# Moving ScalarE's transfers to GpSimd's queue and joining the attention's row loads into one broadcast transfer per operand

## The chip, the cores and the metric

One NeuronCore of a Trainium2 chip runs the whole kernel. The metric is the device time of one execution in microseconds (us); the number for a kernel is the median of its runs. In the names of the profile PE is the matrix engine, DVE is VectorE, ACT is ScalarE, POOL is GpSimd and SP is the SyncE engine, which here only issues transfers. A name with a q behind it (SPq, ACTq, POOLq) is that engine's instruction queue, which also issues the engine's transfers. The transfers themselves run on 16 DMA engines.

## What is computed

One inference step of a decoder layer on 1024 prompt rows and 64 sample rows (8 sequences of 8): a half feed-forward block, a mixing layer, and a second half feed-forward block. The mixing layer joins two parts: softmax attention of 12 heads of width 64, and a gated linear attention. Cut to what matters here (prompt rows):

```python
def _mix_prompt(h, ...):
    qa, ka, va, qb, kb, vb, rb, gk = _project(h, w_in, q_gain, k_gain, w_gk2, b_gk)
    for window, dil in DILATED_BRANCHES:           # (128,1), (512,4), (2048,16)
        o, l = _dilated_prompt(qa, ka, va, rel_bias, window, dil)
    oa = _merge_branches(outs, lses)
    ob, s_fin = _gla(qb, kb, vb, gk, s0, math.gcd(S, GLA_CHUNK))
    y = _merge_out(oa, ob, rb, gla_gain, w_out)
```

The kernel computes the three merged branches of a head as one softmax over all earlier rows, with a bias that holds the relative bias and the count of branches that see a row.

## The kernel before

The program runs in five stages. Times are those of the profiled execution: the first feed-forward block (0 to 788), norms and the projections of the mixing layer with the sample's attention beside them (to about 1244), the prompt's attention with the states of the linear attention beside it (to 1519), the output projection (to 1612), and the second feed-forward block (to the end).

All activations lie transposed, 128 features on the partitions, and every float32 product is made of three products of a high and a low part (`hH`, `hL` and the weights' `hl`). In the projection stage `inputs` runs over 25 units of weights; `turn_values`, `finish_qk` and `finish_gate` bring each unit's result into memory: values to `out_vp`, queries to `qsc`, keys to `out_kT`, the gate to `gsc`. Beside it `sample` computes the sample rows' attention and writes `wk` and `osc`. Before the change SP issues all loads, GpSimd the stores of `qsc` and `out_kT` (L473), and ScalarE all other stores of this stage (L434 to L446, L817, L907).

In `attention` the inner function `load(h)` (L918) brings one head's operands. Each of the query rows (`qsc`) and key rows (`out_kT`) of a head is a block of 64 rows of 1024 numbers, and each is needed twice, on partitions 0 to 63 and on 64 to 127 of a tile `f`:

```python
for w in range(2):
    nc.sync.dma_start(out=f[u][64 * w : 64 * w + 64], in_=src[64 * h : 64 * h + 64])
```

`f` has two buffers, so one for queries and one for keys: the queries of the next head can be loaded only when this head's have been read. VectorE then casts `q` (L932) and `kk` (L934), and GpSimd takes the low parts (L933, L935; VectorE does it for head 0). `bias` comes from `Z` (L937), with two buffers, and `va` (L940) for two heads at a time. `scores` multiplies `kk` by `q` (`psS`, L962) and VectorE makes `e` from it (L969), twelve such instructions a head. `linear_states` loads `g` and `gr` (L596, L598, L643).

Every engine works its instructions off in order. Which order that is, a scheduler decides when the program is built: the generators are interleaved by the costs that they yield (`_interleave`), and the scheduler then places each instruction by its own account of time. Pools that are closed give their memory to later tiles, so a first load of the attention can wait for the last reader of an older tile: `bias` of head 0 lies where the last weights of the projections were, and waits for the last matmul that reads them. Beside such waits a transfer that SP or ACT issues takes one of eight semaphores in turn (DMAHW0 to DMAHW7), and GpSimd's one of eight others (DMASW0 to DMASW7): an issue also waits until the transfer that held its semaphore before has landed.

`sbias` in `sample` (L799) is loaded in the form that the change gives to `f`: 16 rows of memory, repeated 8 times as the leading dimension of the source, onto 128 partitions.

Of the kernel before, what the change touches and what calls it, by code (L numbers as in the profile page):

```python
# [9 lines left out]
F32 = mybir.dt.float32  # L10
# [6 lines left out]
P = 128  # L17
NT = 1088
NP = 1024
# [101 lines left out]
class _Kernel:  # L121
# [299 lines left out]
    def turn_values(self, pool, ps, z, m, ci):  # L421
        nc, a = self.nc, self.a
        cols = slice(128 * m, 128 * m + 128)
        t0, nt = 3 * ci, 3 if ci < 2 else 2
        p = ps.tile([P, 512], F32, tag="b", name="psv")
        for t in range(nt):
            nc.tensor.transpose(p[:, 128 * t : 128 * t + 128], z[:, 128 * t : 128 * t + 128], self.ident)
        if ci == 2:
            nc.tensor.transpose(p[:64, 256:384], z[:, 256:320], self.ident)
        v = pool.tile([P, 3, 128], F32, tag="t1", name="v", bufs=4)  # L430
        nc.scalar.copy(v[:, :nt].rearrange("p t c -> p (t c)"), p[:, : 128 * nt])
        if ci == 2:
            nc.scalar.copy(v[:64, 2], p[:64, 256:384])
            nc.scalar.dma_start(out=self.vnew[:, cols], in_=v[:64, 2])  # L434
            nc.scalar.dma_start(
                out=a["wv_s"].rearrange("b (r c) -> b r c", c=768)[:, 2040:2048, cols], in_=v[:64, 2]
            )
            self.vdone = m + 1
        nc.scalar.dma_start(
            out=a["vp"][128 * t0 : 128 * (t0 + nt), cols].rearrange("(t p) c -> p t c", p=P), in_=v[:, :nt]  # L440
        )

    def finish_gate(self, z, m, ci):
        nc = self.nc
        nc.scalar.activation(z, z, AF.Silu)
        nc.scalar.dma_start(  # L446
            out=self.gsc[3 * ci : 3 * ci + 3, :, 5 + m].rearrange("t p r -> p t r"),
            in_=z.rearrange("p (t r) -> p t r", t=3),
        )
# [131 lines left out]
    def linear_states(self, pool, ps):  # L581

        nc, a = self.nc, self.a
        st = pool.tile([P, 9, 64], F32, tag="st", name="st", bufs=2)
        nc.gpsimd.memset(st[:, 0], 0.0)
        ms = pool.tile([P, 3, 36], F32, tag="gms", name="gms")
        qm = []
        for z in range(2):
            t = pool.tile([P, 4, 8, 32], F32, tag="qm", name="qm", bufs=2)
# [46 lines left out]
        for T in range(9):  # L636
# [11 lines left out]
            for j, src in enumerate((kdT, g[:, 3], g[:, 4])):  # L648
# [3 lines left out]
                out=kx,  # L652
# [125 lines left out]
    def sample(self, pool, ps, loadk):  # L778
# [18 lines left out]
        for i in range(6):  # L797
# [8 lines left out]
            for e in range(2):  # L806
# [9 lines left out]
            nc.scalar.copy(ko, p[:64, :128])  # L816
            nc.scalar.dma_start(  # L817
                out=a["wk"].rearrange("b (r c) -> b r c", c=768)[:, 2040:2048, 128 * i : 128 * i + 128], in_=ko
# [87 lines left out]
            for e in range(2):  # L906
                nc.scalar.dma_start(  # L907
                    out=self.osc[i, 64 * e : 64 * e + 64].rearrange("p (b t) -> p b t", t=8), in_=t[:, :, e]
                )
# [3 lines left out]

    def attention(self, inputs, pool, ps):
        nc = self.nc
        heads = {}

        def load(h):  # L918
            i, e = h // 2, h % 2
            f = []  # L920
            for u, src in enumerate((self.qsc, self.a["kT"])):
                f.append(inputs.tile([P, NP], F32, tag="f", name="f", bufs=2))
                if u == 0:
                    q = inputs.tile([P, NP], F32R, tag="q", name="q", bufs=2)
                    b = inputs.tile([P, NP], F32, tag="bias", name="bias", bufs=2)
                    kk = inputs.tile([P, 2, NP], F32R, tag="kk", name="kk", bufs=2)
                    kh, kl = kk[:, 0], kk[:, 1]
                for w in range(2):
                    nc.sync.dma_start(out=f[u][64 * w : 64 * w + 64], in_=src[64 * h : 64 * h + 64])
            o = slice(64, 128)  # L930
# [6 lines left out]
            nc.sync.dma_start(out=b, in_=bass.AP(z.tensor, z.offset + 127, [[GW - 1, P], [1, NP]]))  # L937
            if e == 0:
                v = pool.tile([P, 8, 128], F32, tag="v", name="va", bufs=2)
                nc.sync.dma_start(  # L940
                    out=v, in_=self.a["vp"][:, 128 * i : 128 * i + 128].rearrange("(t p) c -> p t c", p=P)
                )
            else:
                v = heads[h - 1][3]
            heads[h] = (q, kh, kl, v, b)

        def scores(h, g):

            q, kh, kl, v, b = heads[h]
            out = []  # L950
# [58 lines left out]
        def weigh(h, g, es, pts):  # L1009
            i, e = h // 2, h % 2  # L1010
            r = slice(64 * e, 64 * e + 64)
            v = heads[h][3]
            if g % 2 == 0 and e == 0:
# [26 lines left out]
        self.tc.keep_in_program_order(nc.scalar.preload_act_table_set(LOG_EXP))  # L1040
        load(0)
        yield 10
# [104 lines left out]
    def run(self):  # L1147
        nc, tc, a = self.nc, self.tc, self.a
        self.gready, self.done, self.vdone = False, 0, 0
        with ExitStack() as top:  # L1150
            self.dram = top.enter_context(tc.tile_pool(name="dram", bufs=1, space=DRAM))
# [121 lines left out]
            with ExitStack() as hs:  # L1273
                hpool(hs)
                with ExitStack() as bs:
# [3 lines left out]
                    states = (4.6 * c for c in self.linear_states(gp, ps0))  # L1279
                    _interleave(tc, [(self.attention(ip, ap, ps0), 0), (states, 0)])  # L1280
                with pool("wts") as wp, pool("xp", side="right") as xp:
# [165 lines left out]
```

## Time and profile before

| what | value |
|---|---|
| median of 3 runs | 2398.7 us (2397.25 to 2399.25) |
| the profiled execution's own time | 2401.93 us |
| its span, first to last instruction | 2400.1 us |
| mean granted clock of the matrix engine | 0.989 |
| PE busy over the span | 98% |
| VectorE, ScalarE, GpSimd busy | 48%, 27%, 17% |
| matrix engine's share of the chain that ended last | 89% |

The span is what the trace covers; the execution's own time is 1.8 us longer. The busy shares are averages over five stages, and the change touches only the second and third of them, about a quarter of the span. So the rows below are of those two stages alone.

### The profile page before, as it was taken

Reading aid. Unit: us, or ns where it says so; the run is one execution under the profiler, and the core shown is the slowest. Engines: PE = TensorE matmul, PEld = TensorE weight load, DVE = VectorE, ACT = ScalarE, POOL = GpSimd, SP = SyncE. Lnnn points to the kernel's source line nnn. Section 1 sums busy time; section 2 is a strip of 40 time slices with the busy share of each in tenths; the row PEclk is TensorE's granted clock in tenths of the full one; section 3 lists DMA queues with packets and bytes.
Section 4 is the critical chain, followed back from the end, with each engine's and each line's share of the span. In section 5 each row is a group of like instructions: output and inputs, shape, how many; then the busy total and the mean of one; then the engine's idle time right before and its main releaser. Section 6 shows DMA issues by size and latency. Waiting matters only on the chain.

```text
span 2400.1 us, 38321 instructions
## 1 busy us (share of the span) xinstructions
PE 2341.4 (98%) x16073; PEld 2215.0 (92%) x16073; DVE 1155.9 (48%) x2377; ACT 656.9 (27%) x1347; POOL 408.3 (17%) x303
## 2 busy tenths in 40 slices
PE   7999999999999998999989999999999999999999
PEld 6999999999999987978767767999999999999999
DVE  8452434344342753555538887435444342434333
ACT  5111020101101522545436666334111101020110
POOL 5011020101100400011103231333101101020100
PEclk9999999999999999999999999999999999999999
DMA  7346542524250334599865442414244243111002
GB/s 258 110 162 192 191 152 97 210 97 153 86 196 23 134 131 108 179 342 341 310 184 130 111 115 74 156 36 158 88 163 153 92 154 143 45 53 45 28 17 85
DMA packets 135261, 330.25 MB, mean 138 GB/s; under 512 B 25920, under 2 KB 105264, under 8 KB 127408
## 3 DMA queue, kind: packets, MB, share of 16 engines
q1 hardware_dynamic: 116464, 316.39, 38.7%
q10 hardware_dynamic: 16512, 5.11, 0.9%
q0 software_dynamic: 2112, 6.29, 0.7%
q8 instruction: 126, 2.06, 0.3%
q14 instruction: 47, 0.39, 0.0%
HBM read 300.55 MB, written 134.56 MB: 181 GB/s over the span
## 4 chain that ended last, share of the span: by engine, by line
PE 89%; DVE 5%; DMA 3%; ACT 2%; issue 1%; SPq 1%; POOL 0%; ACTq 0%; DVEq 0%; POOLq 0%
PE ps L306 42%; PE ps L257 21%; PE psg L306 12%; PE pso L306 4%; PE psO L1022 2%; PE psS L962 2%; PE psW L880 1%; PE psT L1001 1%; DMA vt<-in_vin 1%; PE psA L831 1%; DVE hL L155 1%; DVE e L969 1%; PE pss L459 1%; DMA f<-out_kT 0%; DVE rstd L170 0%
## 5 line engine op out<-in xcount | busy, mean ns | idle before, releaser
L306 PE MATMUL ps<-hH,hl 128*128 128x362 f32 (+1 forms) x4224 | 1044.1, 328 | 8.1 <-ACT hl L130 6.8
L306 PEld LDWEIGHTS ps<-hH,hl 128*128 128x128 f32 x4224 | 746.6, 188 | 12.4 <-ACT hl L130 6.7
L306 PE MATMUL ps<-hL,hl 128*128 128x362 f32 (+1 forms) x2112 | 691.5, 328 | 2.9 <-DVE hL L155 2.9
L257 PE MATMUL ps<-g,hl 128*128 128x362 f32 (+1 forms) x3168 | 529.2, 328 | 0.0
L257 PEld LDWEIGHTS ps<-g,hl 128*128 128x128 f32 x3168 | 527.0, 188 | 0.0
L134 POOL TENSOR_TENSOR hl<-raw,hl 128x1024 fp32r<-128x1024 f32 (+1 forms) x98 | 242.8, 2498 | 1223.3 <-ACT hl L130 1223.3
L306 PEld LDWEIGHTS ps<-hL,hl 128*128 128x128 f32 x2112 | 397.5, 188 | 4.9 <-DVE hL L155 3.9
L306 PE MATMUL psg<-hH,hl 128*128 128x384 f32 (+3 forms) x1200 | 312.4, 334 | 0.0
L262 DVE SCALAR_TENSOR_TENSOR xT<-ps,xT 128x362 f32<-128x362 f32 (+1 forms) x384 | 204.6, 534 | 200.3 <-PE ps L257 191.4
L217 ACT ACTIVATE t<-t 128x364 f32<-128x364 f32 x132 | 66.9, 508 | 786.0 <-DVE t L216 785.8
L218 DVE TENSOR_TENSOR t<-ps,rstd 128x364 f32<-128x364 f32 x132 | 70.6, 535 | 417.9 <-PE ps L306 417.9
L306 PEld LDWEIGHTS psg<-hH,hl 128*128 128x128 f32 (+1 forms) x1200 | 211.3, 186 | 12.8 <-issue 8.9
L306 PE MATMUL psg<-hL,hl 128*128 128x384 f32 (+3 forms) x600 | 200.1, 334 | 0.1
L130 ACT CAST hl<-raw 128x1024 fp32r<-128x1024 f32 (+2 forms) x148 | 124.1, 886 | 187.3 <-PE ps L306 109.9
L130 ACT CAST g<-t 128x364 fp32r<-128x364 f32 x132 | 65.2, 494 | 346.8 <-DVE t L219 346.8
L134 DVE TENSOR_TENSOR g<-t,g 128x364 fp32r<-128x364 f32 x132 | 107.1, 813 | 92.8 <-ACT g L130 92.5
L216 DVE TENSOR_TENSOR t<-ps,rstd 128x364 f32<-128x364 f32 x132 | 70.5, 535 | 156.6 <-PE ps L306 155.3
L306 PEld LDWEIGHTS psg<-hL,hl 128*128 128x128 f32 (+1 forms) x600 | 111.7, 186 | 9.3 <-issue 6.7
L134 DVE TENSOR_TENSOR hl<-raw,hl 128x384 fp32r<-128x384 f32 (+3 forms) x178 | 102.9, 587 | 23.9 <-ACT hl L130 19.9
L962 PE MATMUL psS<-kk,q 128*128 128x512 f32 (+2 forms) x288 | 92.2, 411 | 19.6 <-DVE s L969 11.9
L306 PE MATMUL pso<-hH,hl 128*128 128x362 f32 (+1 forms) x384 | 93.6, 325 | 0.2 <-DVE o L1032 0.2
L982 ACT ACTIVATE e<-e,s 128x128 f32<-128x128 f32 (+3 forms) x96 | 74.9, 780 | 43.7 <-DVE s L969 43.1
(205 smaller groups left out, 2007.2 us busy)
## 6 DMA issues: line engine op xcount, KB each, us to landing
out_wk<-in_ck SPq DMA_DIRECT2D x16, 3060.0 KB
out_wv_s<-in_cv SPq DMA_DIRECT2D x16, 3060.0 KB
kt<-in_kin SPq DMA_DIRECT2D x24, 1280.0 KB
vt<-in_vin SPq DMA_DIRECT2D x60, 512.0 KB
raw<-in_w13b SPq DMA_DIRECT2D x22, 1024.0 KB
raw<-in_w13a SPq DMA_DIRECT2D x21, 1024.0 KB
raw<-in_w2a SPq DMA_DIRECT2D x48, 192.0 KB
raw<-in_w2b SPq DMA_DIRECT2D x48, 192.0 KB
```

Of the source, the lines that this page charges most:

```text
L130: nc.scalar.copy(hi, x)
L134: e.tensor_tensor(out=lo, in0=x, in1=hi.bitcast(F32), op=ALU.subtract)
L155: nc.vector.scalar_tensor_tensor(out=self.hL[:, k, s], in0=x, scalar=g, in1=self.hH[:, k, s].bitcast(F32), op0=ALU.mult, op1=ALU.subtract)
L216: nc.vector.tensor_tensor(out=t1[:, :n], in0=p1[:, :n], in1=r, op=ALU.mult)
L217: nc.scalar.activation(t1[:, :n], t1[:, :n], AF.Silu)
L218: nc.vector.tensor_tensor(out=t3[:, :n], in0=p3[:, :n], in1=r, op=ALU.mult)
L257: self.mm(p[:, :n], lhsT=hl[:, wt, j, :], rhs=g[:, gp, :n], start=i == 0, stop=i == 3 * nf - 1)
L262: nc.vector.scalar_tensor_tensor(out=xs, in0=p[:, :n], scalar=0.5, in1=xs, op0=ALU.mult, op1=ALU.add)
L306: self.mm(p[:m, :n], lhsT=hl[:, wt, k, cs], rhs=h[:, k, h0 : h0 + n], start=i == 0, stop=i == 23)
L962: self.mm(p[:, :mm], lhsT=q[:, 128 * n : 128 * n + 128], rhs=kk[:, o : o + mm], start=x == 0, stop=x == 1,)
L982: nc.scalar.activation(e[:, :w], e[:, :w], AF.Exp, scale=-1.0, bias=s[:, j : j + 1], accum_out=s[:, 2:3])
L1022: self.mm(p[64 * n : 64 * n + 64, :128], lhsT=v[:, k, r], rhs=pts[k // 2][k, n], start=k == 0, stop=k == 2 * g + n, tile_position=(0, 64 * n),
```

## The change

Every transfer that ScalarE issued is now issued by GpSimd: 54 of them (18 of `out_vp`, 6 each of `vnew`, `out_wv_s`, `out_wk` and `gsc`, 12 of `osc`). In `load(h)` the two transfers of an operand become one whose source repeats the 64 rows: in the built program the source's dimensions are [2 (step 0), 64, 1024] and the destination's [128, 1, 1024]. The loads of `va` move into `load_v`, their tile into the pool of the linear states, the first one ahead of the states' work. Head 0's load is recorded with a higher priority, and the states are interleaved ahead of the attention.

```diff
--- before.py
+++ after.py
@@ -431,19 +431,19 @@
         nc.scalar.copy(v[:, :nt].rearrange("p t c -> p (t c)"), p[:, : 128 * nt])
         if ci == 2:
             nc.scalar.copy(v[:64, 2], p[:64, 256:384])
-            nc.scalar.dma_start(out=self.vnew[:, cols], in_=v[:64, 2])
-            nc.scalar.dma_start(
+            nc.gpsimd.dma_start(out=self.vnew[:, cols], in_=v[:64, 2])
+            nc.gpsimd.dma_start(
                 out=a["wv_s"].rearrange("b (r c) -> b r c", c=768)[:, 2040:2048, cols], in_=v[:64, 2]
             )
             self.vdone = m + 1
-        nc.scalar.dma_start(
+        nc.gpsimd.dma_start(
             out=a["vp"][128 * t0 : 128 * (t0 + nt), cols].rearrange("(t p) c -> p t c", p=P), in_=v[:, :nt]
         )
 
     def finish_gate(self, z, m, ci):
         nc = self.nc
         nc.scalar.activation(z, z, AF.Silu)
-        nc.scalar.dma_start(
+        nc.gpsimd.dma_start(
             out=self.gsc[3 * ci : 3 * ci + 3, :, 5 + m].rearrange("t p r -> p t r"),
             in_=z.rearrange("p (t r) -> p t r", t=3),
         )
@@ -583,6 +583,7 @@
         nc, a = self.nc, self.a
         st = pool.tile([P, 9, 64], F32, tag="st", name="st", bufs=2)
         nc.gpsimd.memset(st[:, 0], 0.0)
+        self.load_v(pool, 0)
         ms = pool.tile([P, 3, 36], F32, tag="gms", name="gms")
         qm = []
         for z in range(2):
@@ -814,7 +815,7 @@
             nc.tensor.transpose(p[:64, :128], ks, self.ident)
             ko = pool.tile([64, 128], F32, tag="sko", name="sko", bufs=1)
             nc.scalar.copy(ko, p[:64, :128])
-            nc.scalar.dma_start(
+            nc.gpsimd.dma_start(
                 out=a["wk"].rearrange("b (r c) -> b r c", c=768)[:, 2040:2048, 128 * i : 128 * i + 128], in_=ko
             )
             e = pool.tile([P, NKEY], F32, tag="se", name="se", bufs=1)
@@ -904,14 +905,21 @@
             t = pool.tile([64, 8, 2, 8], F32, tag="soT", name="soT", bufs=1)
             nc.scalar.copy(t, p[:64, :128].rearrange("p (b e t) -> p b e t", e=2, t=8))
             for e in range(2):
-                nc.scalar.dma_start(
+                nc.gpsimd.dma_start(
                     out=self.osc[i, 64 * e : 64 * e + 64].rearrange("p (b t) -> p b t", t=8), in_=t[:, :, e]
                 )
             yield 100
 
 
 
-    def attention(self, inputs, pool, ps):
+    def load_v(self, pool, i):
+        v = pool.tile([P, 8, 128], F32, tag="v", name="va", bufs=2)
+        self.nc.sync.dma_start(
+            out=v, in_=self.a["vp"][:, 128 * i : 128 * i + 128].rearrange("(t p) c -> p t c", p=P)
+        )
+        self.values[i] = v
+
+    def attention(self, inputs, pool, vpool, ps):
         nc = self.nc
         heads = {}
 
@@ -925,8 +933,9 @@
                     b = inputs.tile([P, NP], F32, tag="bias", name="bias", bufs=2)
                     kk = inputs.tile([P, 2, NP], F32R, tag="kk", name="kk", bufs=2)
                     kh, kl = kk[:, 0], kk[:, 1]
-                for w in range(2):
-                    nc.sync.dma_start(out=f[u][64 * w : 64 * w + 64], in_=src[64 * h : 64 * h + 64])
+                nc.sync.dma_start(
+                    out=f[u], in_=src[64 * h : 64 * h + 64].unsqueeze(0).broadcast_to([2, 64, NP])
+                )
             o = slice(64, 128)
             el = nc.gpsimd if h else nc.vector
             nc.vector.tensor_copy(q, f[0])
@@ -935,18 +944,16 @@
             el.tensor_tensor(out=kl, in0=f[1], in1=kh.bitcast(F32), op=ALU.subtract)
             z = self.Z[h]
             nc.sync.dma_start(out=b, in_=bass.AP(z.tensor, z.offset + 127, [[GW - 1, P], [1, NP]]))
-            if e == 0:
-                v = pool.tile([P, 8, 128], F32, tag="v", name="va", bufs=2)
-                nc.sync.dma_start(
-                    out=v, in_=self.a["vp"][:, 128 * i : 128 * i + 128].rearrange("(t p) c -> p t c", p=P)
-                )
-            else:
-                v = heads[h - 1][3]
-            heads[h] = (q, kh, kl, v, b)
+            if h % 2 == 0 and h:
+                load_v(i)
+            heads[h] = (q, kh, kl, b)
+
+        def load_v(i):
+            self.load_v(vpool, i)
 
         def scores(h, g):
 
-            q, kh, kl, v, b = heads[h]
+            q, kh, kl, b = heads[h]
             out = []
             ss = pool.tile([P, 2, 4], F32, tag="s", name="s", bufs=6)
             for n in (2 * g, 2 * g + 1):
@@ -1009,7 +1016,7 @@
         def weigh(h, g, es, pts):
             i, e = h // 2, h % 2
             r = slice(64 * e, 64 * e + 64)
-            v = heads[h][3]
+            v = self.values[i]
             if g % 2 == 0 and e == 0:
                 outs[i, g // 2] = pool.tile([P, 512], F32, tag="o", name="o", bufs=3)
             p = ps.tile([P, 512], F32, tag="O", name="psO", bufs=2)
@@ -1038,7 +1045,8 @@
         lag = 3
         outs = {}
         self.tc.keep_in_program_order(nc.scalar.preload_act_table_set(LOG_EXP))
-        load(0)
+        with self.tc.high_priority(offset=300):
+            load(0)
         yield 10
         es = {}
         for x in range(len(order) + lag):
@@ -1147,6 +1155,7 @@
     def run(self):
         nc, tc, a = self.nc, self.tc, self.a
         self.gready, self.done, self.vdone = False, 0, 0
+        self.values = {}
         with ExitStack() as top:
             self.dram = top.enter_context(tc.tile_pool(name="dram", bufs=1, space=DRAM))
             cp = top.enter_context(tc.tile_pool(name="const", bufs=1))
@@ -1277,7 +1286,7 @@
                     ap = bs.enter_context(pool("att", side="right"))
                     ps0 = bs.enter_context(pool("ps", space=PSUM))
                     states = (4.6 * c for c in self.linear_states(gp, ps0))
-                    _interleave(tc, [(self.attention(ip, ap, ps0), 0), (states, 0)])
+                    _interleave(tc, [(states, 0), (self.attention(ip, ap, gp, ps0), 0)])
                 with pool("wts") as wp, pool("xp", side="right") as xp:
                     w = _Weights(self, wp, [a["wout"][u] for u in range(4)] + w13b)
                     w.start()
```

What this makes of the order on SP's queue, where the projections end and the attention's loads begin. Before (in brackets: the semaphores that a row waits for; a name without DMA is an engine's; `f_11121` and `f_11127` are the queries and keys of head 0, `f_11163` the queries of head 1):

```order
L794 DMA vt_10909<-in_vin 128x1024 [waits PE_49]
L940 DMA va_11135<-out_vp 128x8x128 [waits DMAHW5_49,DVE_49,Pool_49]
L940 DMA va_11349<-out_vp 128x8x128 [waits DMAHW6_49,Activation_49]
L929 DMA f_11121<-qsc_66 64x1024 [waits DMASW2_49,DMAHW0_49,DMASW1_49,DMASW0_49]
L929 DMA f_11121<-qsc_66 64x1024 [waits DMAHW1_49]
L929 DMA f_11127<-out_kT 64x1024 [waits DMASW5_49,DMAHW2_49,DMASW4_49,DMASW3_49]
L929 DMA f_11127<-out_kT 64x1024 [waits DMAHW3_49]
L937 DMA bias_11123<-Z_73 128x1024 [waits DMAHW4_49,PE_49]
L596 DMA g7_11144<-gsc_68 128x640 [waits DMAHW5_49]
L598 DMA g7_11144<-asc_69 128x4x128 [waits DMAHW6_49]
L937 DMA bias_11165<-Z_73 128x1024 [waits DMAHW7_49,PE_49]
```

And now (`f_11133` and `f_11138` are head 0's queries and keys, `f_11161` head 1's queries):

```order
L795 DMA vt_10909<-in_vin 128x1024 [waits DMAHW7_49,DMAHW0_49,PE_49]
L936 DMA f_11133<-qsc_66 128x1x1024 [waits DMASW2_49,DMASW3_49,DMASW1_49,DVE_49]
L936 DMA f_11138<-out_kT 128x1x1024 [waits DMASW6_49,DMAHW1_49,DMASW5_49,DMASW4_49]
L946 DMA bias_11135<-Z_73 128x1024 [waits DMAHW2_49,PE_49]
L917 DMA va_11122<-out_vp 128x8x128 [waits DMAHW3_49]
L597 DMA g7_11129<-gsc_68 128x640 [waits DMAHW4_49,Pool_49]
L599 DMA g7_11129<-asc_69 128x4x128 [waits DMAHW5_49]
L946 DMA bias_11163<-Z_73 128x1024 [waits DMAHW6_49,PE_49]
L597 DMA g7_11288<-gsc_68 128x640 [waits DMAHW7_49]
L599 DMA g7_11288<-asc_69 128x4x128 [waits DMAHW0_49]
L644 DMA gr_11292<-gsc_68 128x3x256 [waits DMAHW1_49,DMASW4_49,DMASW2_49]
L936 DMA f_11161<-qsc_66 128x1x1024 [waits DMAHW2_49,DVE_49]
```

Head 0's loads stand directly behind the last load of the sample's values and no longer behind `va`; their waits are for the stores of `qsc` and `out_kT` and for an old reader of their memory. The load of `gr` waits for the semaphore DMAHW1 that head 0's keys held, and head 1's queries stand behind it; the next two rows are the second `va` and head 1's keys.

On VectorE's queue, the second cast of head 1 before (the names `e` are head 0's scores):

```order
L932 CAST q_11164<-f_11163 128x1024
L969 ISA e_11194,s_11193<-psS_11195,bias_11123 128x512
L969 ISA s_11193 128x1
L989 RECIPROCAL s_11177<-s_11177 128x2
L651 TENSOR_TENSOR kx_11302<-psR_11298,cmask_469 128x1024
L969 ISA e_11194,s_11193<-psS_11199,bias_11123,s_11193 128x128
L969 ISA s_11193 128x1
L934 CAST kk_11166<-f_11169 128x1024
```

And now:

```order
L941 CAST q_11162<-f_11161 128x1024
L1039 TENSOR_TENSOR o_11240<-psO_11315,rb_11317 64x128 x2
L976 ISA e_11220,s_11219<-psS_11221,bias_11135 128x512
L976 ISA s_11219 128x1
L996 RECIPROCAL s_11189<-s_11189 128x2
L976 ISA e_11220,s_11219<-psS_11225,bias_11135,s_11219 128x384
L976 ISA s_11219 128x1
L677 SCALAR_TENSOR_TENSOR st_11120<-st_11120,gbl_11278,psD_11358 128x64
L943 CAST kk_11164<-f_11166 128x1024
```

The casts of head 1 moved back from after 4 and 6 of head 0's twelve scores to after 8 and 10. Those of head 2 moved from after 11 scores of head 0 to after 12 and 14. From head 3 on they stand, as before, at the end of the scores of two heads earlier: VectorE reaches the scores of head n-1 only behind the casts of head n.

## Rows read from the trace of the kernel before

**Rows 1.** The page: busy us, share of the span and instructions of each engine.

```profile
PE 2341.4 (98%) x16073; PEld 2215.0 (92%) x16073; DVE 1155.9 (48%) x2377; ACT 656.9 (27%) x1347; POOL 408.3 (17%) x303
```

**Rows 2.** Busy by stretch: from:to, length, engines, PE clock, DMA share, GB/s.

```profile
940.00:1240.00 300.00, 288.00 (x2246) 241.05 (x2245) 142.79 (x294) 129.19 (x274) 29.61 (x80) 0.98 0.78 266
1240.00:1278.00 38.00, 25.66 (x198) 19.25 (x198) 25.05 (x69) 18.14 (x46) 12.48 (x10) 0.79 0.76 198
1278.00:1519.00 241.00, 226.37 (x2734) 177.80 (x2732) 192.07 (x586) 164.68 (x437) 59.95 (x42) 0.97 0.37 102
```

**Rows 3.** Timeline of PE, 1243 to 1252: start, us, operation [idle before <-releaser].

```profile
1243.59 0.31 PE L306 MATMUL psg<-hH,hl 128*128 128x320 f32 x1
1250.82 0.77 PE L962 MATMUL psS<-kk,q 128*128 128x256 f32 x2 [6.91 <-DVE kk L934]
```

**Rows 4.** Timeline of SP's queue, 1220 to 1250.

```profile
1224.89 1.75 SPq L794 DMA_DIRECT2D vt<-in_vin  x4
1237.09 1.01 SPq L940 DMA_DIRECT2D va<-out_vp  x2
1238.26 6.00 SPq L929 DMA_DIRECT2D f<-qsc  x2
1245.28 1.11 SPq L929 DMA_DIRECT2D f<-out_kT  x2
1246.50 0.53 SPq L937 DMA_DIRECT2D bias<-Z  x1
```

**Rows 5.** Timeline of SP's queue, 1125 to 1150.

```profile
1133.35 0.62 SPq L799 DMA_DIRECT2D sbias<-sB  x1
1145.30 3.92 SPq L794 DMA_DIRECT2D vt<-in_vin  x6
```

**Rows 6.** Busy by stretch, microsecond by microsecond, around that sbias transfer.

```profile
1138.20:1139.20 1.00, 1.00 (x8) 1.00 (x7) 0.45 (x1) 0.51 (x1) 0.00 (x0) 1.00 1.08 368
1139.20:1140.20 1.00, 1.00 (x9) 0.97 (x8) 0.11 (x1) 0.00 (x0) 0.00 (x0) 1.00 0.50 131
1140.20:1141.20 1.00, 1.00 (x9) 1.00 (x8) 0.00 (x0) 0.59 (x2) 0.00 (x0) 1.00 0.50 146
1141.20:1142.20 1.00, 1.00 (x9) 1.00 (x8) 0.56 (x1) 0.97 (x3) 0.00 (x0) 1.00 0.50 202
```

**Rows 7.** Transfers issued between 1240 and 1520: tile, queue, count, KB each.

```profile
f<-out_kT SPq DMA_DIRECT2D x24, 256.0 KB
bias<-Z SPq DMA_DIRECT2D x12, 512.0 KB
...
g<-gsc SPq DMA_DIRECT2D x9, 320.0 KB
g<-asc SPq DMA_DIRECT2D x9, 256.0 KB
va<-out_vp SPq DMA_DIRECT2D x4, 512.0 KB
...
gr<-gsc SPq DMA_DIRECT2D x3, 384.0 KB
```

**Rows 8.** GpSimd's low parts of a head, by tile f: duration ns min/median/max, first and last.

```profile
L933 POOL TENSOR_TENSOR q<-f,q x11: 2347/2603/2714, 1262.0 to 1473.5; 64x1024 fp32r<-64x1024 f32 x11
L935 POOL TENSOR_TENSOR kk<-f,kk x11: 2367/2430/2501, 1265.5 to 1476.2; 128x1024 fp32r<-128x1024 f32 x11
```

**Rows 9.** The chain of waits, 1260 to 1275: start, us, what.

```profile
1268.46 3.81 DMA f<-out_kT
```

**Rows 10.** Timeline of VectorE: the first score, and casts of kk for heads 1, 2, 3, 11.

```profile
1253.04 0.28 DVE L969 CUSTOM_DVE_ANT_0 e<-psS,bias 128x128 f32<-128x128 f32 x1
...
1264.71 0.69 DVE L934 CAST kk<-f 128x1024 fp32r<-128x1024 f32 x1 [0.91 <-issue]
...
1272.37 2.61 DVE L934 CAST kk<-f 128x1024 fp32r<-128x1024 f32 x1 [0.42 <-DMA f<-out_kT]
...
1294.37 0.69 DVE L934 CAST kk<-f 128x1024 fp32r<-128x1024 f32 x1
...
1473.18 0.69 DVE L934 CAST kk<-f 128x1024 fp32r<-128x1024 f32 x1
```

**Rows 11.** GpSimd's groups, 826 to 1240: count | busy us, mean ns | idle before.

```profile
L473 POOL DMA_DIRECT2D qsc<-z x18 | 10.0, 554 | 143.0 <-DVE z L468 143.0
```

## Prediction

> **What bounds the kernel now.** I read the page first. The matrix engine is busy for 98% of the span [rows 1], so a gain has to come out of its few gaps, and a loss out of new ones. Then busy time by stretch [rows 2]: in the projections (940 to 1240) PE is busy 288.00 of 300 us, in the prompt's attention (1278 to 1519) 226.37 of 241; between them, 1240 to 1278, only 25.66 of 38, at a granted clock of 0.79. So the projections hold at most 12.0 us, and the step into the attention 12.3. The timeline of PE shows that step [rows 3]: the last projection matmul starts at 1243.59, the first score matmul (psS) at 1250.82, and PE sat idle for 6.91 us until a cast of kk was done. SP's queue shows why [rows 4]: free since 1226.64, it issued va only at 1237.09, and head 0's query rows took it 6.00 us to issue, as each stood behind transfers that shared their semaphores; the key rows went out at 1245.28. That is the stall the change goes for.
>
> **The removed waits.** Head 0's rows now stand behind the vt of 1224.89 [rows 4], so SP can issue them at about 1227 instead of 1238 and 1245. Bias cannot come so early: its memory is read by the last projection matmul, 1243.9 [rows 3]. It would be issued at 1244.2 instead of 1246.50, so the first score could at best move from 1253.04 [rows 10] to about 1250: 3 us. Everything now depends on how long the new transfers take.
>
> **The new transfers.** No transfer of the trace repeats its source twice, but sbias repeats it 8 times in the same form. SP issued one at 1133.35 and nothing more until 1145.30 [rows 5]; once the kt load ahead of it was through, the 16 DMA engines were busy for a share of 1.08, and then, with sbias alone in flight, for 0.50, 0.50 and 0.50 [rows 6]. Exactly half, for three microseconds: the transfer ran on 8 engines, as many as its source's leading dimension. A source that leads with 2 I therefore take to run on 2 engines. The Trainium skill says the same in DMA: Bandwidth & Descriptors, Rules for kernel authors: a leading zero-stride broadcast of c copies keeps a transfer on at most c engines. By that rule, which speaks against this change, the sum is the one below, and the half share agrees with it.
>
> One operand is 512 KB, two of the present 256 KB [rows 7], so 256 KB an engine. An engine's rate is 202/8 = 25.3 GB/s in the fastest of the three microseconds [rows 6], and (131+146+202)/3/8 = 20.0 in their mean. That is 10.4 us or 13.1 us an operand. I take 10.4, since two engines that ask for the same rows are nearer to an undisturbed one than eight are; 13.1 stays for the range. The other traffic puts a sixteenth on every engine. Per head, bias is 512 KB, va 512 for two heads, nine g of 320+256 and three gr of 384 for twelve heads [rows 7]: 512+256+432+96 = 1296 KB, or 81 KB an engine, 3.3 us. So the two busy engines need 2*10.4+3.3 = 24.1 us a head. Now a head takes (1473.18-1294.37)/8 = 22.4 us [rows 10]. The load becomes the bound, if both operands use the same two engines. No row tells which engines a small transfer gets; that one queue always starts at the same one is the simplest reading, and I take it (the other is a rival). The Trainium skill (DMA: Bandwidth & Descriptors, Why a DMA increments its semaphore by 16 and not by 1) says that such transfers get the lowest-numbered engines; no run here shows it.
>
> **The first heads.** I assume that an engine works one queue's shares off in order. The vt of 1224.89 are through by about 1232. Queries of head 0: to 1242.4; keys: to 1252.8, landed 1254.3. (Fixed part of a transfer, 2.5 us: one key load landed 3.81 us after its issue [rows 9], less 1.3 for the 512 KB of its pair at 25.3 GB/s on 16 engines; I put 1 us of it ahead of the data and 1.5 behind.) With cast and low part (about 2) and the matmul (0.8) the first score is at 1257, not 1253.04 [rows 10]: **+4**.
>
> Head 1's queries stand behind gr, which waits for the semaphore that head 0's keys hold until 1254.3; meanwhile bias, va, two pairs of g, bias and gr (3072 KB, 7.8 us an engine) have queued up. Queries: 1260.6 to 1271.0; va 1.3; keys to 1282.7, landed 1284.2, where the cast of kk was at 1264.71 [rows 10]: **+19.5**. VectorE stands at that cast, with the last scores of head 0 behind it. Head 2's queries may go when GpSimd has read head 1's (2.60 us, [rows 8]): issued 1276, on the engines 1282.7 to 1293.1; its keys follow bias to 1304.8, landed 1306.3 for 1272.37: **+34**. Head 3's: queries to 1316.6, keys to 1327.0, landed 1328.5 for 1294.37: **+34**.
>
> **Every further head.** Let T be when VectorE casts q of head n, C when it casts kk. GpSimd's part ends 0.7+2.6 after T; issue 0.5, 1 us to the first data, 20.8 for both operands, 3.3 for the rest, 1.5 to land: the next C is T+30.4. The next T is C+21.8, the scores between (22.4 less the cast). Two heads take 30.4+21.8 = 52.2 us, a head 26.1, more than the 24.1 of the engines alone, since the single buffer lets them idle. From C = 1328.5 and T = 1325.7 for head 3 (T: ten of head 1's scores, 10/12*22.4, behind head 2's cast), head 11 comes at 1328.5+4*52.2 = 1537.3, where it was 1473.18: +64. Two heads are left behind that cast, as before, so the stage ends **64 us later**.
>
> **The moved stores.** ScalarE sheds 54 issues; it is busy 129.19 of 300 us there and PE 288.00 [rows 2], so PE hides that. GpSimd takes them at some 0.55 us each [rows 11], 30 us beside 29.61 busy. In its order the stores of queries and keys now stand behind others that wait for ScalarE; those 18 of queries waited 143.0 us in all for VectorE [rows 11], so GpSimd has about 8 us of slack before each. If that cover went, the z tiles would stay full and PE would stand. Gain and loss are both bounded by the stretch's 12.0 idle us; I take 0, as 96% busy leaves little either way. The order of states and attention costs nothing by itself: both wait for the same loads.
>
> **Sum.** The profiled execution took 2401.93 us, 1.8 more than its span and 3.2 over the median of the runs; with +64 it is 2466. From the median, 2398.7+64 = **2463**.
>
> **Rivals.**
> 1. *The transfer spreads over all engines.* Against it stands the half share [rows 6]; for it, that a destination of 128 partitions could be what counts. The Trainium skill (DMA: Bandwidth & Descriptors, Rules for kernel authors) advises one 128-partition transfer in place of two halves; by that rule alone the time would be this rival's. Head 0's rows land by 1232, bias alone decides, the first score comes at 1250, and the gap [rows 3] shrinks by 3 us: 2396, faster. It decides if an operand lands within the 21.8 us for which VectorE is busy with a head. Small gains in the projections (up to 12) could add to it. Chance 0.11.
> 2. *Two engines, but other ones for each transfer.* Then queries and keys go side by side. A later C is at T+30.4-10.4 = T+20.0, under the 21.8 of the scores: hidden. What stays is the start: head 2's keys wait for GpSimd's part of head 1 and for bias, which waits for head 0's last scores at about 1273; issued 1274, landed 1287 for 1272.37, and head 3 ten scores later, 1306 for 1294.37: +11, **2410**. Chance 0.07.
> 3. *The forecast.* Chance 0.82.
>
> **Range and chances.** A measurement of this kernel can tell about 0.2%, 4.8 us, from no change. The forecast's own bounds: with engines that never idle, 24.1 a head, and some 25 at the start, 25+8*1.7 = +39, 2438; with 13.1 us an operand two heads take 57.6, so 8*6.4 = +51, and the five transfers up to head 3 add 13 to +34, so +98, 2497. With up to 12 from the stores either way the ends are about 2425 and 2505; this leaves out the rivals (0.18) and little else. A clock that falls in the new gaps, as to 0.79 in [rows 2], lies inside the upper half. Slower: forecast and rival 2, 0.89. Rival 1's 2396 lies near the limit: faster 0.06, same 0.05.
>
> **What would show it.** Right: with f alone in flight a DMA share near 2/16 = 0.12, long stretches of it between 1240 and 1580; VectorE idle before the casts of q and kk on the transfers of f; casts some 26 us apart; the first score later than now; the second half of the program unchanged, only shifted. Wrong: f landing within some 5 us at a high share (rival 1), or casts 22.4 us apart behind a late start (rival 2). A loss in the projections, with PE waiting there, would show that the stores were costed wrongly.

## The result, and the profile after

The changed kernel takes **2494.17 us** (median of 6 runs, 2492.71 to 2497.29); the kernel before, beside it, 2398.97 us (6 runs, 2397.25 to 2402.19). The ratio is 1.0395, 95% interval 1.0382 to 1.0409: **slower by 95 us**. The forecast was 2463, its range 2425 to 2505. The sign, the place and the main mechanism came as forecast; two terms of the sum did not.

Stage by stage, from:to, length, busy time of the engines, granted clock, DMA share and GB/s. The kernel before:

```profile
940.00:1244.00 304.00, 291.90 (x2271) 244.66 (x2269) 143.41 (x297) 130.65 (x277) 29.61 (x80) 0.98 0.78 267
1244.00:1519.00 275.00, 248.13 (x2903) 193.44 (x2903) 216.50 (x653) 181.36 (x479) 72.42 (x52) 0.94 0.41 112
1612.00:2400.00 788.00, 784.76 (x4762) 783.76 (x4760) 326.01 (x598) 125.65 (x207) 117.80 (x54) 1.00 0.26 93
```

The changed kernel:

```profile
940.00:1234.00 294.00, 291.05 (x2262) 242.32 (x2260) 143.03 (x296) 131.00 (x278) 54.59 (x118) 1.00 0.79 274
1234.00:1609.00 375.00, 265.50 (x2903) 205.82 (x2903) 206.15 (x653) 179.16 (x478) 71.50 (x53) 0.83 0.26 83
1702.00:2490.00 788.00, 784.83 (x4763) 783.83 (x4761) 326.38 (x598) 125.72 (x207) 117.69 (x55) 1.00 0.26 93
```

Read the lengths. The projections end 10 us earlier. The attention takes 375 us for 275, and VectorE, ScalarE and GpSimd are busy no longer than before: what was added is waiting. The last block is the same, only shifted. The two profiled spans differ by 2490.9 - 2400.1 = 90.8 us, and -10 and +100 make that up.

The rows that answer to [rows 3], [rows 4] and [rows 10]. Timeline of PE, the last projection matmul (psg), the first score matmul and the first matmul of the output projection (pso):

```profile
1233.68 0.31 PE L306 MATMUL psg<-hH,hl 128*128 128x320 f32 x1
1247.75 0.80 PE L969 MATMUL psS<-kk,q 128*128 128x256 f32 x2 [13.76 <-DVE kk L943]
...
1608.38 0.43 PE L306 MATMUL pso<-hH,hl 128*128 128x364 f32 x1
```

And the last of these in the kernel before, where [rows 3] has the first:

```profile
1518.30 0.43 PE L306 MATMUL pso<-hH,hl 128*128 128x364 f32 x1
```

Timeline of SP's queue, head 0's rows and bias:

```profile
1217.33 0.57 SPq L936 DMA_DIRECT2D f<-qsc  x1
1218.06 0.53 SPq L936 DMA_DIRECT2D f<-out_kT  x1
1230.54 0.78 SPq L946 DMA_DIRECT2D bias<-Z  x1
```

Timeline of VectorE, casts of kk (heads 0 to 5, and 11) and the first score, with the idle time before them:

```profile
1247.00 0.69 DVE L943 CAST kk<-f 128x1024 fp32r<-128x1024 f32 x1 [9.61 <-DMA f<-out_kT]
1249.63 0.29 DVE L976 CUSTOM_DVE_ANT_0 e<-psS,bias 128x128 f32<-128x128 f32 x1 [0.67 <-DMA f<-qsc]
1276.62 0.69 DVE L943 CAST kk<-f 128x1024 fp32r<-128x1024 f32 x1 [8.67 <-DMA f<-out_kT]
1298.60 0.69 DVE L943 CAST kk<-f 128x1024 fp32r<-128x1024 f32 x1 [9.57 <-DMA f<-out_kT]
1320.77 0.69 DVE L943 CAST kk<-f 128x1024 fp32r<-128x1024 f32 x1 [5.97 <-DMA f<-out_kT]
1355.14 0.69 DVE L943 CAST kk<-f 128x1024 fp32r<-128x1024 f32 x1
1392.40 0.69 DVE L943 CAST kk<-f 128x1024 fp32r<-128x1024 f32 x1
...
1561.68 0.69 DVE L943 CAST kk<-f 128x1024 fp32r<-128x1024 f32 x1 [6.66 <-DMA f<-out_kT]
```

SP issues head 0's rows in a microsecond, at 1217 instead of 1238 to 1246; they still land some 13 us after PE has nothing left. Heads 1 to 3 come 22 us apart. Then two gaps of 34.4 and 37.3 us, before casts that wait for no row of their own. Who waited there tells the list of waits, VectorE, 1234 to 1610 (total, times, longest):

```profile
DVE kk L943 <- DMA f<-out_kT: 55.1, 9, 9.6
DVE gw L612 <- DMA g<-gsc: 47.4, 5, 17.2
...
DVE q L941 <- DMA f<-qsc: 14.4, 3, 6.8
```

and ScalarE in the same stretch:

```profile
ACT hH L130 <- DMA so<-osc: 17.5, 1, 17.5
```

The kernel before has this line for g, VectorE, 1244 to 1519:

```profile
DVE gw L611 <- DMA g<-gsc: 7.1, 5, 3.4
```

So 40 us more of waiting for `g`, a transfer that the change did not touch, and 17.5 for `so`, another. Stretches of the changed kernel show why: first rows of `f` alone in flight (from 1325 on the queries issued at 1317.41 and the keys issued at 1324.32, both together); then around the `g` that SP issued at 1329.82:

```profile
1302.00:1312.00 10.00, 10.00 (x104) 8.46 (x106) 7.58 (x25) 6.37 (x18) 0.46 (x1) 0.89 0.13 53
...
1325.00:1327.00 2.00, 2.00 (x17) 1.62 (x14) 0.36 (x2) 0.78 (x2) 0.00 (x0) 0.50 0.13 53
...
1330.80:1332.30 1.50, 1.50 (x30) 0.91 (x29) 0.61 (x3) 0.63 (x1) 0.00 (x0) 1.00 0.94 286
1332.30:1333.50 1.20, 1.20 (x30) 1.11 (x29) 0.70 (x2) 0.29 (x2) 0.00 (x0) 1.00 0.90 173
1334.00:1341.00 7.00, 1.00 (x7) 0.57 (x5) 0.00 (x0) 0.00 (x0) 0.00 (x0) 0.81 0.13 53
1341.00:1344.50 3.50, 0.00 (x0) 0.00 (x0) 0.30 (x2) 0.35 (x2) 0.00 (x0) 0.50 0.09 34
```

A share of 0.13 is two engines of 16, for 10 us on end, and no more than two while queries and keys are both in flight. `g` comes: for 2.7 us nearly all engines run, then two again, for `f`, and only in the last of these stretches the rest of `g`. VectorE and ScalarE, which stood for `g`, start at 1344.1. Fourteen engines had done their share of it nearly 11 us before.

My theory after this profile (A): the loss is the broadcast's, in two parts, the rows that are late themselves and the transfers whose share stands behind them on the two engines. A rival (B): the new order puts the states' loads into the way, and the broadcast costs only its own throughput. For the 10 us gained: the stores (A), or the new order (C).

### The profile page after: what moved, and what is told of

Same layout as the page of the kernel before. It is cut to its first block, busy times and chain, and to the rows that moved or that the text cites. A ratio compares the mean times of both kernels' runs of the same rounds, so it can differ in the third digit from the quotient of the medians.

```text
span 2490.9 us, 38329 instructions
## 1 busy us (share of the span) xinstructions
PE 2358.1 (95%) x16073; PEld 2225.3 (89%) x16073; DVE 1141.9 (46%) x2377; ACT 655.5 (26%) x1347; POOL 442.3 (18%) x357
## 4 chain that ended last, share of the span: by engine, by line
PE 83%; DMA 10%; DVE 3%; issue 1%; POOL 1%; ACT 1%; SPq 0%; POOLq 0%; DVEq 0%; ACTq 0%
PE ps L306 41%; PE ps L257 20%; PE psg L306 11%; DMA f<-out_kT 7%; PE pso L306 4%; PE psA L832 1%; PE psW L881 1%; DMA so<-osc 1%; PE psO L1029 1%; DVE hL L155 1%; DMA g<-gsc 1%; PE psS L969 1%; POOL kk L944 1%; DMA vt<-in_vin 1%; PE psT L1008 1%
## 5 line engine op out<-in xcount | busy, mean ns | idle before, releaser
L969 PE MATMUL psS<-kk,q 128*128 128x512 f32 (+2 forms) x288 | 98.8, 435 | 67.6 <-DVE s L976 53.3
L969 PEld LDWEIGHTS psS<-kk,q 128*128 128x128 f32 x288 | 49.9, 215 | 82.9 <-DVE s L976 49.4
L1008 PE MATMUL psT<-ident,e 128*128 128x128 f32 x432 | 75.1, 303 | 24.6 <-ACT gsq L721 13.3
```

Source lines behind the costliest of these rows:

```text
L969: self.mm(p[:, :mm], lhsT=q[:, 128 * n : 128 * n + 128], rhs=kk[:, o : o + mm], start=x == 0, stop=x == 1,)
L1008: nc.tensor.transpose(p[:, j], es[n][:, 128 * k : 128 * k + 128], self.ident)
```

## The experiments

**1. Two halves again.** The changed kernel with one edit:

```diff
-                nc.sync.dma_start(
-                    out=f[u], in_=src[64 * h : 64 * h + 64].unsqueeze(0).broadcast_to([2, 64, NP])
-                )
+                for w in range(2):
+                    nc.sync.dma_start(out=f[u][64 * w : 64 * w + 64], in_=src[64 * h : 64 * h + 64])
```

> The changed kernel with the rows of queries and keys again in two transfers of 64 rows each; everything else of the change stays. Theory A (the whole loss is the broadcast transfer: 10.6 us on two DMA engines for each operand, and on those two engines whatever stands behind it): the projections end at about 1234 us as in the changed kernel, the attention takes 270 to 276 us as before, the time is 2386 to 2391 us, below both kernels. Theory B (the new order, states first and head 0's loads ahead, carries a good part of the loss of the attention): above 2400 us, with VectorE still waiting 20 us or more for g.

Measured: 2386.75 us (2382.73 to 2390.87), ratio to before 0.9945 (0.9928 to 0.9962): **faster than both kernels**, than the one before by half a per cent. In the profiled execution, the shortest of the four (2382.73), the attention lasts from 1234.6 to 1498.8, 264 us, 6 us under what A expected. VectorE's wait for g:

```profile
DVE gw L612 <- DMA g<-gsc: 7.9, 4, 3.4
```

Back at its old size, in the new order. B falls: the new order is not what costs the time.

**2. The broadcast alone.** The same edit turned round, in the kernel before.

> The kernel before with one edit: one broadcast transfer for each operand. Theory A: the attention takes some 100 us more, the projections keep their 12 idle us, 2490 to 2508 us. Theory B: the loss is partly that of the order, so the transfer alone costs what its two engines need by themselves, 24 to 26 us a head against 22.4: 2415 to 2440 us.

Measured: 2511.25 us, ratio 1.0464 (1.0449 to 1.0480), 3 us above the range of A. Its attention takes 110 us more than the kernel before, not 100: the broadcast alone carries the whole loss. Timeline of PE, first score matmul:

```profile
1266.48 0.77 PE L963 MATMUL psS<-kk,q 128*128 128x256 f32 x2 [23.03 <-DVE kk L935]
```

PE stands 23.03 us here and 13.76 in the changed kernel: the early issue of head 0's rows is worth 9.3 us once the transfer is slow.

**3. The stores alone.** The kernel before with `nc.gpsimd.dma_start` in place of its six `nc.scalar.dma_start`.

> The kernel before with one edit: the 54 stores that ScalarE issued are issued by GpSimd. Theory A (ScalarE stood 17 us in front of one store, behind a semaphore that a transfer of SP's queue held, and PE 8.8 us behind ScalarE): the projections end 9 to 10 us earlier, PE's wait of 8.8 us for ScalarE's copy of v is gone, 2387 to 2392 us. Rival C (the 10 us come from the new order of loads): 2397 to 2401 us.

Measured: 2391.68 us (2388.78 to 2398.83), ratio 0.9963 (0.9950 to 0.9975), as A had it. What was removed stands in the kernel before, ScalarE's timeline, where its queue (ACTq) issues one store 17 us after the copy ahead of it:

```profile
937.04 0.26 ACT L433 COPY v<-psv 64x128 f32<-64x128 f32 x1
954.63 0.38 ACTq L439 DMA_DIRECT2D out_vp<-v  x1
...
957.51 0.48 ACT L431 COPY v<-psv 128x384 f32<-128x384 f32 x1 [20.20 <-DMA vt<-in_vin]
```

and in the list of PE's waits, 930 to 1244, of the kernel before:

```profile
PE psv L427 <- ACT v L431: 8.8, 1, 8.8
```

In the built program that store waits for a semaphore last taken by SP's load of `sbias`, which SP issued only between 941 and 945; the next stores wait for the mask's and vt's. Behind the store stood the copy for which PE waited. GpSimd's stores take semaphores of their own, and that line is in neither the changed kernel's list nor this one's. In the profiled execution here (2398.83, the longest of the six) the projections end 4.6 us earlier, not 10: PE waits 3.3 us for vt, where it waits 1.1 in the kernel before, which is a part of the difference; the rest stays open. The median says 9.2.

**4. The states' loads on another queue.** The changed kernel with

```diff
-            nc.sync.dma_start(out=g[:, :5], in_=self.gsc[T, :, :5])
+            nc.scalar.dma_start(out=g[:, :5], in_=self.gsc[T, :, :5])
```

and so the second transfer of `g` and that of `gr`.

> The changed kernel with the loads of the linear states (g and gr, 21 transfers) issued by ScalarE, so on another DMA queue. Theory A1 (they are late because they stand behind the broadcasts in the same queue on the same two engines; another queue is served in turn): VectorE's wait for g falls from 47 to under 15 us, a head takes about 26 us, the time is 2455 to 2475 us. Theory A2 (the two engines are simply full, whichever queue): the wait for g stays above 35 us, 2485 to 2505 us.

Measured: 2476.81 us, ratio 1.0320 (1.0304 to 1.0335), 2 us above A1's range and 8 below A2's. The two lines, VectorE's and ScalarE's:

```profile
DVE gw L612 <- DMA g<-gsc: 19.2, 5, 4.7
```

```profile
ACT hH L130 <- DMA so<-osc: 19.0, 1, 19.0
```

The wait for g falls from 47.4 to 19.2, its longest from 17.2 to 4.7. One `g` as ScalarE issues it and VectorE first uses it, and the two stretches behind that use:

```profile
1331.97 0.34 ACTq L597 DMA_DIRECT2D g<-gsc  x1
```

```profile
1338.62 0.29 DVE L612 TENSOR_TENSOR gw<-g 128x128 f32<-128x128 f32 x1 [3.35 <-DMA g<-gsc]
```

```profile
1338.60:1341.00 2.40, 1.43 (x19) 1.29 (x21) 2.34 (x8) 2.38 (x9) 0.62 (x1) 0.94 0.13 50
...
1342.00:1343.00 1.00, 1.00 (x9) 0.67 (x7) 0.47 (x2) 0.82 (x3) 0.00 (x0) 0.50 0.13 51
```

From issue to use it is 6.7 us, against 14.3 for the `g` of 1329.82 in the changed kernel, and the queries and keys that SP had issued before it (1321.23 and 1326.28) still run on two engines for 4 us after it: a transfer on another queue does not stand behind the whole broadcast. A1 was right in kind, though the wait stayed 4 us over its bound; `so`, still on SP's queue, stayed late.

**5. Only the queries by broadcast**, the keys in two halves.

> The changed kernel with the broadcast for the queries alone; the keys come in two transfers of 64 rows. If two engines need 10.6 us an operand (theory A), a head asks them for 10.6 + 3.3 us, less than the 21 us of its scores, so the pace is that of the scores; what stays is g, so and the keys' own shares on those two engines, up to 10 us late behind the queries: VectorE waits 5 to 20 us for g, 2390 to 2415 us. If the loss goes with the number of broadcasts (each costs by its issue or its semaphore): half of it, 2435 to 2450 us.

Measured: 2442.85 us, ratio 1.0171 (1.0156 to 1.0186). The time is that of the second case, half of the loss. Its cause is not: VectorE's waits, 1234 to 1640:

```profile
DVE gw L612 <- DMA g<-gsc: 36.4, 5, 10.0
...
DVE q L945 <- DMA f<-qsc: 20.6, 3, 10.8
```

The rows of `f` are waited for by the first three heads alone, as A says: from the fourth on the queries land while VectorE works. What remains is g, some 8 to 10 us each time but the first, about as long as one operand holds the two engines. A's number was wrong by the same term as the prediction's: a load that is itself hidden makes others late. The second case's cause, a price of each broadcast by its issue or its semaphore, is refuted by the tenth experiment, which issues as many transfers and loses nothing.

**6. The keys' broadcast on ScalarE's queue.**

```diff
-                nc.sync.dma_start(
+                (nc.sync, nc.scalar)[u].dma_start(
```

> The changed kernel with the keys' broadcast issued by ScalarE, so on another DMA queue. If both queues put such a transfer on the same two engines (theory A, as in the prediction), the packets of queries and keys stay at two in flight together, the pair takes 21 us as before, 2465 to 2500 us. If the other queue puts it on another pair (the prediction's second rival by another road), four are in flight, a head's rows land within 11 us: 2400 to 2440 us.

Measured: 2488.27 us, ratio 1.0362 (1.0346 to 1.0377). A stretch in which both queues have a broadcast in flight (queries issued 1279.83, keys 1283.27; their casts come at 1297.46 and 1305.03, and both waited for them):

```profile
1291.00:1296.00 5.00, 0.00 (x0) 0.00 (x0) 0.00 (x0) 0.00 (x0) 0.00 (x0) 0.50 0.13 52
```

Two engines for two queues, 52 GB/s for both. The prediction's choice, the same two engines for each such transfer, holds in one queue (the stretch from 1325 above), and across queues too. The Trainium skill (DMA: Bandwidth & Descriptors, Rules for kernel authors) says that spreading transfers over SP, ACT and GpSimd doesn't help bandwidth, since all use the same engines; this row agrees. The fourth experiment shows a case in which a second queue does help: for a transfer that is late, and not slow.

**7. Two real copies.** GpSimd stores the queries twice; the source of their transfer leads with 2, at a stride of 3 MB in place of 0.

```diff
-            self.qsc = d([768, NP], F32, name="qsc")
+            self.qsc = d([2, 768, NP], F32, name="qsc")
...
+                    nc.sync.dma_start(out=f[u], in_=src[:, 64 * h : 64 * h + 64])
```

> The changed kernel with the queries stored twice (18 more stores by GpSimd), so that their transfer has the same leading dimension of 2, but with a stride of 3 MB in place of 0; the keys keep the broadcast. If the leading dimension of 2 decides (theory A as the prediction put it), the queries' 512 KB still take 10.6 us on two engines: 2485 to 2505 us. If the zero stride decides, the queries spread over all engines (about 2 us, a share near 1) and the loss is that of one broadcast: 2390 to 2420 us.

Measured: 2504.52 us, ratio 1.0429 (1.0414 to 1.0445). A stretch with the queries' transfer alone in flight (issued 1272.66, the keys' at 1284.10):

```profile
1274.50:1283.00 8.50, 1.45 (x8) 0.93 (x6) 2.09 (x7) 1.03 (x2) 1.29 (x1) 0.67 0.13 54
```

Two engines again: it is not the zero stride. What is left is the leading dimension of 2, which the tenth experiment takes away. The Trainium skill (DMA: Bandwidth & Descriptors, Why a DMA increments its semaphore by 16 and not by 1) gives the rule in this form: the slowest dimension that is not 1 sets the number of engines. The trace agrees, with 0.13.

**8. No raised priority.** The first experiment with a plain `load(0)`.

> The first experiment (two transfers of 64 rows) without the raised priority of head 0's loads; states first and the va tile in the states' pool stay. The attention of the first experiment took 10 us less than that of the kernel before, 3.7 of them ahead of the first score. If the priority is worth just those 3.7: the first score comes 7 us behind the last projection instead of 3.5, 2389 to 2393 us. If it carries all 10: 2395 to 2399 us. If none: 2385 to 2388 us.

Measured: 2387.57 us, ratio 0.9942 (0.9925 to 0.9959), against 0.9945 for the first experiment: no difference that can be told. PE does wait 7.16 us for the first score instead of 3.23, and in the profiled executions the attention takes 268.9 us instead of 264.2; but the four executions of the first experiment lie up to 8 us apart and its profile is of the shortest, so a gain of 4 us is neither shown nor refuted. With short loads the early issue is worth nothing measurable here; the second experiment shows that with long ones it is. What the rest of the new order brings (first against third experiment, 0.9945 and 0.9963) lies within the intervals.

**9. so off the queue too.** The fourth experiment, with

```diff
-                    nc.sync.dma_start(out=t, in_=self.osc.rearrange("i p t -> p i t"))
+                    nc.gpsimd.dma_start(out=t, in_=self.osc.rearrange("i p t -> p i t"))
```

> The fourth experiment (g and gr issued by ScalarE) with the load of so, the samples' attention output, issued by GpSimd, so that it too leaves the queue of the broadcasts. In the fourth, ScalarE still stood 19.0 us for so, and PE and VectorE 15.0 behind ScalarE. If a transfer is late only because it stands behind 21 us of broadcast in its queue: that wait falls under 5 us, the time by 8 to 18 us, 2458 to 2469 us. If so is late for another reason (its stores, or the two engines full on every queue): the wait stays above 12 us, 2473 to 2480 us.

Measured: 2466.26 us (2461.69 to 2467.88), ratio 1.0282 (1.0265 to 1.0300), within the range. The last projection matmul and the first of the output projection, here and in the fourth experiment:

```profile
1234.50 0.31 PE L306 MATMUL psg<-hH,hl 128*128 128x320 f32 x1
...
1577.65 0.43 PE L306 MATMUL pso<-hH,hl 128*128 128x364 f32 x1
```

```profile
1236.23 0.31 PE L306 MATMUL psg<-hH,hl 128*128 128x320 f32 x1
...
1592.07 0.43 PE L306 MATMUL pso<-hH,hl 128*128 128x364 f32 x1
```

ScalarE's wait, VectorE's, and casts of kk for heads 5 and 11:

```profile
ACT hH L130 <- DMA so<-osc: 2.1, 1, 2.1
```

```profile
DVE kk L943 <- DMA f<-out_kT: 62.4, 12, 11.4
```

```profile
1373.53 0.69 DVE L943 CAST kk<-f 128x1024 fp32r<-128x1024 f32 x1 [5.41 <-DMA f<-out_kT]
...
1531.52 0.69 DVE L943 CAST kk<-f 128x1024 fp32r<-128x1024 f32 x1 [4.71 <-DMA f<-out_kT]
```

158.0 us for six heads are **26.3 us a head**, where the prediction's recurrence gave 26.1. With these other transfers out of the way, it is the queries' and keys' own loads that set the pace: VectorE waits for the keys at each of the twelve heads.

**10. One transfer of 128 real rows.** The queries are stored twice per head, one copy behind the other, in four stores instead of one; their one transfer leads with 128. Keys in halves, as in the fifth.

```diff
-            self.qsc = d([768, NP], F32, name="qsc")
+            self.qsc = d([12, 128, NP], F32, name="qsc")
...
+                    nc.sync.dma_start(out=f[u], in_=src[h])
```

> As the fifth experiment (one transfer for the queries, two of 64 rows for the keys), but GpSimd stores each head's queries twice, one behind the other, in four stores in place of one, so that the one transfer of 128 rows has 128 as its leading dimension. If the leading dimension of the source decides how many engines run: the queries land in some 4 us at a share near 1, VectorE waits under 10 us for g, 2384 to 2395 us, against 2442.85 for the fifth. If a transfer to 128 partitions, or a single one for each operand, is slow by itself: 2430 to 2450 us. The 54 more stores of GpSimd may cost up to 10 us in the projections.

Measured: 2386.43 us, ratio 0.9944 (0.9929 to 0.9958), some 55 us less than the fifth. A stretch behind the issue of such a transfer at 1299.75:

```profile
1300.70:1303.00 2.30, 2.30 (x29) 1.96 (x28) 2.15 (x9) 2.30 (x8) 1.72 (x2) 1.00 0.76 228
```

Same bytes, same 128 partitions, one transfer: share 0.76 instead of 0.13. So the source's leading dimension decides. The number of transfers is not the matter either; one big one gains nothing over two halves (0.9944 and 0.9945).

## Why the prediction was right, and where not

1. **Two engines an operand: right.** Share 0.13 was forecast as 0.12. The 53 GB/s of that stretch make 9.9 us for 512 KB, where I took 10.4 and kept 13.1 for the range. Experiments 7 and 10 give the reason as taken: the source's leading dimension.
2. **The same two for both operands: right**, a choice without a row then, now shown by the changed kernel itself (0.13 from 1325 to 1327, with both operands in flight) and across queues by experiment 6. Rival 1 fell with the share, rival 2 with these two stretches.
3. **The first heads: right but for their start.** Heads 1, 2 and 3 were forecast at 1284.2, 1306.3 and 1328.5, and came at 1276.6, 1298.6 and 1320.8. Each is 7.6 to 7.7 us early, as the projections ended 9.9 us early; the two steps between them are right within 0.2 us. For the same reason the first score came at 1249.63, not at 1257, and so earlier than the 1253.04 of before, though "later than now" was one of the signs. Counted from the end of the last projection matmul it did come later, by 15.6 us for 9.1. One reading of that part was wrong without consequence: bias did not wait for the last projection matmul (SP issued it at 1230.54, the matmul starts at 1233.68).
4. **Every further head: the step that failed.** Forecast were 26.1 us a head, (1561.68 - 1320.77)/8 = 30.1 came. "3.3 for the rest" counted the other transfers as work of the two engines, and that is all that was counted. Not counted: the wait for a transfer that is itself made late. A transfer over 16 engines is done only when its shares on those two are, behind up to two operands, and VectorE and ScalarE stand in their order at the first use of `g` and `so`. Taking both out of the queue (experiment 9) brings the attention, from the end of the last projection matmul to the first of the output projection, from 374.4 us to 342.8, and the pace to 26.3. The kernel before has 274.4. So of the 100 us, 342.8 - 274.4 = 68 are those that I forecast as 64, and some 32 the missing term: 19 for `g` and `gr` (fourth experiment: 355.5), 13 for `so`. The split is not exact: in experiment 9 VectorE still waits 19.6 us for `g`, where it waits 7.1 in the kernel before, and no run shows whether that costs time there. What it costs ScalarE and GpSimd to issue them themselves is inside these numbers.
5. **The moved stores: 0 forecast, 10 us gained.** "96% busy leaves little either way" was right as a bound of 12 us, and the choice within it wrong. I read in [rows 4] that SP's transfers wait for each other's semaphores, and did not look for the same on ScalarE, where 8.8 of the 12.0 idle us of [rows 2] were one such wait. Experiment 3 gives 9.2.
6. **Sum.** -10 (stores) + 68 + 32 = +90, the spans' 90.8. The missing 10 and 32 have opposite signs, so the forecast missed the spans' difference by 27 us (that of the medians by 31), and not by 37. That the time lies inside the range is in part luck: its upper half was kept for slower operands (13.1 us), dearer stores and a lower clock, not for this wait, and of the three only the lower clock came. Everything after the attention was only shifted, as forecast.

Left open: how much the lower granted clock in the attention (0.83 for 0.94) adds by itself. PE is busy there for 265.50 us instead of 248.13 with the same 2903 matmuls, but no run separates this from the waits. A third and fourth buffer for `f`, which might take the coupling out of the recurrence, were not tried, as the memory beside the other tiles has no room for them.

## What to carry to other kernels

Look at the source's outermost dimension of each transfer before joining two: if it is 2, two engines carry it, whatever its stride and however many partitions it fills. Price such a transfer twice: once for those who need it, and once for every transfer behind it in its queue, of which two sixteenths can be late by up to its whole length. And where an engine that computes also issues transfers, look for the gap between its copy and its store: a semaphore shared with another queue's transfer holds up everything behind it.

## What was not expected of the hardware

- A `g` that was seven eighths through after 2.7 us held VectorE and ScalarE for 11 us more, for its shares on two engines. In the fifth experiment VectorE waited 20.6 us for the broadcast itself, at the first three heads, and never after; against the first experiment it still cost some 55 us.
- Two queues do not bring two pairs of engines: with a broadcast in flight on each, the share stayed 0.13 and the rate 52 GB/s.
- A real second copy, 3 MB further on, ran no faster than the zero stride (0.13 and 54 GB/s against 0.13 and 53).
